# Down-projection of a two-layer decoder trunk: seven pairs of chunks by seven products in two passes

## The chip, the core and the metric

The kernel runs on one core of a Trainium2 chip. TensorE (PE) multiplies, VectorE (DVE), ScalarE (ACT) and GpSimd (POOL) work elementwise, SyncE (SP) and POOL issue DMAs. Every engine takes its instructions in program order and waits on semaphores. The metric is device time in microseconds (us), here the median of three runs: 1158.79 us (1158.62 to 1159.23).

## The reference

A decoder trunk of two layers over 512 tokens of width 1024 in float32: attention, then a gated ConvFFN, each between two RMS norms. What matters here is the ConvFFN, which runs once in each layer:

```
def conv_ffn(xn, w_up, cw, cb, w_down):
    a = xn @ w_up                       # 512 x 5632
    ...                                 # causal depthwise conv of width 3
    gate, val = jnp.split(a, 2, axis=-1)
    return (jax.nn.gelu(gate, approximate=True) * val) @ w_down   # 512 x 2816 @ 2816 x 1024
```

## The kernel before

**Splits.** Each float32 operand is split into a high part (rounded to float32r by ACT) and a low part (operand minus high part, by DVE). A product of two operands is three matmuls (`mm3`, L235 to L238): high by high, high by low, low by high. Class `Weights` (L27) loads weight pieces of 128x1024 in a fixed order (`pieces`), always `ahead_dma` pieces ahead, by DMAs on SP (L41); `high` (L45) is the ACT copy (L49), `low` (L52) the DVE subtraction (L55); `take` hands out pieces that aren't split.

**Up stage.** `ffn` (L509) works through 22 chunks (NF) of 128 rows of the gated width; a chunk needs two pieces of `w_up` (gate and value half). A plain chunk is 48 matmuls of 128x512 (`up`). Chunks in `SEVEN` (6, 8, ..., 20) compute the product of 2x2 blocks by seven products in place of eight: 84 matmuls of 128x256 (`prod`), with sums on DVE (`csum`, L671, L672, and L679 to L686) between them, and `seven_weights` makes their operands two chunks ahead. `weights(c + 2)` is a generator whose steps are put between TensorE's products (`next(steps)`). When TensorE is done with a chunk, `post` runs its taps (`taps`, the convolution: ACT L535, DVE L536 and L538 for each half), the GELU (`glu`, L554), and, a chunk later, `product`, which multiplies gate and value into `hc` and stores it to `hD` in DRAM by a DMA on SP (L549).

**Down projection.** `Proj(NF, 4, get_act).finish` (L322, L351): for each of the 22 chunks (`kc`), for four blocks of 128 tokens (`b`) and two halves of 512 columns (`hf`), `mm3` adds to one of eight PSUM banks (`acc`), which takes all eight banks. A chunk is 24 matmuls of 128x512. The last four chunks are run block by block, so that the boundary (norms, next stage) can start. `load_h` and `prep` (L512, L518) load two chunks of `hD` and split them (`hs`, L523, L524). While chunks 20 and 21 of the up stage run, `weights(22)` and `weights(23)` split the first four pieces of `w_down`, and `prep(0)`, `prep(1)` the first activations.

**Buffers.** `t8` has 17 buffers of 8 KB a partition (split weights `w`, `hs`, `xT`), `t4` 9 of 4 KB (raw weights `wraw`, `bb`, `hraw`), `t2` 6 of 2 KB. A buffer is free for the next tile once all that read or write it is done; the order on each engine is the order of the program.

Of the kernel before, what the change touches and what calls it, by code (L numbers as in the profile page):

```python
# [16 lines left out]
NB = 4  # L17
# [4 lines left out]
EPS = 1e-6  # L22
NEG = -1e30
BIG = 3.0e38


class Weights:  # L27
# [31 lines left out]
    def take(self, k):  # L59

        self.load(self.n_split + k + self.ahead_dma)
        raws = [self.raw.pop(self.n_split + i) for i in range(k)]
        self.n_split += k
        return raws

    def split(self, n):
        while self.n_split < min(n, len(self.pieces)):
# [10 lines left out]
def trunk_kernel(ctx, tc, x, norm_gains, w_qkv_a, w_o_a, w_q_b, w_o_b, kv_norm, w_kvf, b_f,  # L78
# [52 lines left out]
    def add_rows(w, n):  # L131
        for kc in range(n):
            add(lambda raw, kc=kc: [(raw, w[kc * 128:(kc + 1) * 128, :])])

    def add_cols(w, c):
# [2 lines left out]
    def add_ffn(l):  # L138
        for c in range(NF):
            add_cols(w_up[l], c * 128)  # L140
            add_cols(w_up[l], DFF + c * 128)
        add_rows(w_down[l], NF)

    add_rows(w_o_a[0], 6)
    add_ffn(0)
    for hf in range(2):
        for s in range(4):
# [6 lines left out]
                add_cols(w_kvf, c * 128)  # L154
    for c in range(1, 8):
        add_cols(w_q_b[0], c * 128)
    add_rows(w_o_b[0], 8)
    add_ffn(1)

    early = []  # L160
# [100 lines left out]
    class Mix:  # L261


        def __init__(self, gain):
            self.gain, self.st = gain, {}
# [56 lines left out]
    class Proj:  # L322

        def __init__(self, KC, R, get_act):
            self.KC, self.R, self.get_act = KC, R, get_act
            self.w, self.banks, self.done = {}, {}, set()

        def weight(self, kc):  # L330
            while len(self.w) <= kc:
                self.w[len(self.w)] = W.get()
            return self.w[kc]

        def step(self, kc, b, hf, part=slice(0, 512)):
            ah, al = self.get_act(kc)
            w = self.weight(kc)
            s = slice(b * 128, b * 128 + 128)
            c = slice(hf * 512 + part.start, hf * 512 + part.stop)
            if kc == 0:  # L340
                self.banks[b, hf] = bank([128, 512], name="acc")
            mm3(self.banks[b, hf][:, part], ah[:, s], al[:, s], w[0][:, c], w[1][:, c],
                kc == 0, kc == self.KC - 1, part.start > 0)

        def both(self, kc, b):
            if (kc, b) not in self.done:
# [4 lines left out]
        def finish(self, bd, ahead, hook=None):  # L351
            n = self.KC - self.R
            if hook is None:
                for kc in range(n):
# [149 lines left out]

    SEVEN = range(6, NF - 1, 2)

    def ffn(bd, cp, nxt, ahead):  # L509
        hD = tc.dram_tile([NF, 128, T], F32, name="hD")  # L510
# [2 lines left out]
        def load_h(j):  # L513
            if j < NF // 2:
                hraw[j] = t4([128, 2, T], name="hraw")
                sp.dma_start(hraw[j], hD[2 * j:2 * j + 2].rearrange("c p t -> p c t"))

        def prep(j):  # L518
            if j < NF // 2:
                load_h(j + 1)  # L520
                hs[j] = t = t8([128, 2, 2, T], F32R, name="hs")
                src = hraw.pop(j)
                act.copy(t[:, 0], src)  # L523
                dve.tensor_tensor(t[:, 1], src, t[:, 0].bitcast(F32), ALU.subtract)  # L524
# [3 lines left out]
                prep(kc // 2 + 1)  # L528
            return hs[kc // 2][:, 0, kc % 2], hs[kc // 2][:, 1, kc % 2]

        def taps(c, banks):
            bb = t4([128, 2, T], name="bb")
            for s, ch in ((0, c), (1, NF + c)):
                ps = banks[s]
                act.activation(bb[:, s, :], ps, AF.Identity, bias=cp[:, 3, ch:ch + 1], scale=cp[:, 2, ch:ch + 1])  # L535
                dve.scalar_tensor_tensor(bb[:, s, 1:], ps[:, :T - 1], cp[:, 1, ch:ch + 1], bb[:, s, 1:],  # L536
                                         ALU.mult, ALU.add)
                dve.scalar_tensor_tensor(bb[:, s, 2:], ps[:, :T - 2], cp[:, 0, ch:ch + 1], bb[:, s, 2:],  # L538
                                         ALU.mult, ALU.add)
            return bb  # L540

        gated = []

        def product():

            if gated:
                c, bb = gated.pop()
                if c - 1 in hc:
                    sp.dma_start(hD[c - 1], hc.pop(c - 1))  # L549
                hc[c] = t2([128, T], name="hc")  # L550
                dve.tensor_tensor(hc[c], bb[:, 0, :], bb[:, 1, :], ALU.mult)
# [5 lines left out]
        def post(c, banks):  # L557
            product()
            glu(c, taps(c, banks))

        xT = None
        XA, XB = [], []
# [54 lines left out]
        def plain_weights():  # L617
            for _ in range(2):
                W.high()
                W.low()  # L620
                yield

        def weights(c):
            return seven_weights(c) if c in SEVEN else plain_weights()

        def half_mm(o, w, x, s, start):
            for k in range(4):
# [16 lines left out]
        begun = None  # L644
        before = None
        for c in range(2, NF):
            if c == NF - 2:
                load_h(0)
            if c == NF - 1:
                prep(0)  # L650
                prep(1)
            steps = weights(c + 2)
            banks = [bank([128, T], name="up") for _ in range(2)]
            if c in SEVEN:
                w = halves.pop(c)
                W.n_get += 2
                x11, x21, x22 = [(xT[0][i], xT[1][i], s) for i, s in ((0, LO), (1, LO), (1, HI))]
                o1, o2, o3, o4 = banks[0][:, LO], banks[0][:, HI], banks[1][:, LO], banks[1][:, HI]
                s1, s12, s17 = (t2([128, 256], name="csum") for _ in range(3))

                def prod(o, a, x, start=False):
                    half_mm(o, w[a], x[0:2], x[2], start)

                prod(o1, "A11", x11, True)
# [6 lines left out]
                dve.tensor_tensor(s12, o2, s1, ALU.add)  # L671
                dve.tensor_tensor(s17, o3, s1, ALU.add)  # L672
# [12 lines left out]
                next(steps, None)  # L685
                dve.tensor_tensor(o2, o2, s1, ALU.add)  # L686
            else:
                for s in range(2):
                    if s == 0 and begun:
                        w, banks[0] = begun  # L690
                        up(*begun, range(4, KD))
                        begun = None
                    else:
                        up(W.get(), banks[s], range(KD))
                    if s == 0 and before:
                        post(*before)
                    next(steps, None)
                    next(extra, None)
            for _ in steps:
                pass  # L700
            before = c, banks
        post(*before)
        product()
        sp.dma_start(hD[NF - 1], hc.pop(NF - 1))

        W.ahead = 4
        Proj(NF, 4, get_act).finish(nxt, ahead)

# [690 lines left out]
```

## Time and profile before

| | |
|---|---|
| median of three runs | 1158.79 us |
| the profiled execution, time / span | 1158.71 us / 1156.9 us |
| DVE, ACT, POOL busy over the span | 66%, 48%, 11% |
| down projection, layers 0 and 1, first acc matmul | at 419 us and 1033 us |
| DMA, mean over the span | 120 GB/s, 138.90 MB |

A row of the timeline gives start, duration, engine, line and operation, output and inputs; in brackets, how long the engine was idle before it and what it waited for. In a group row, x is the count. A window row gives each engine's busy us (and instructions), the granted clock (PEclk, 1.00 is full), the share of the DMA engines and GB/s.

### The profile page before, as it was taken

The page shows a single profiled execution, that of the slowest core. Times are in us where ns is not written, and L with a number is a line of the kernel's source. Part 1 is how long each engine was busy: PE and PEld are TensorE (multiplying, and loading weights), DVE is VectorE, ACT ScalarE, POOL GpSimd, SP SyncE. Part 2 cuts the span into 40 slices and gives each one's busy share as a digit, 9 for nine tenths or more (in the row PEclk, how much of TensorE's full clock was granted, in tenths as well). Part 3 has the DMA queues.
Part 4 walks back from the last instruction along what each step waited for, and adds up shares of the span by engine and source line. Part 5 has one row for each costly group of instructions (what it writes and reads, how often), then busy time and mean ns, then how long its engine had stood idle before and what let it go on. Part 6 is the DMA issues. An engine that isn't in the chain of part 4 may idle for free.

```text
span 1156.9 us, 16648 instructions
## 1 busy us (share of the span) xinstructions
PE 1142.1 (99%) x6474; PEld 977.5 (84%) x6474; DVE 767.1 (66%) x1227; ACT 554.9 (48%) x956; POOL 131.5 (11%) x191
## 2 busy tenths in 40 slices
PE   9999999999999999999999999999999999999997
PEld 6888889888998888888778888789888998888886
DVE  6433488888878766306564788758788888867204
ACT  5444565444445545305452677755454444445202
POOL 2722003000000000000000565502100000000000
PEclk9999999999999999999999999999999999999999
DMA  8131064334344449203304344274334434539001
GB/s 295 56 111 37 2 173 123 101 110 143 112 127 140 154 158 375 75 1 78 89 1 129 101 118 126 77 203 128 101 92 129 145 105 143 169 124 379 1 1 73
DMA packets 147176, 138.90 MB, mean 120 GB/s; under 512 B 6809, under 2 KB 120969, under 8 KB 147098
## 3 DMA queue, kind: packets, MB, share of 16 engines
q1 hardware_dynamic: 145818, 133.64, 36.7%
q0 software_dynamic: 1280, 4.20, 1.6%
q8 instruction: 51, 0.84, 0.3%
q14 instruction: 27, 0.22, 0.1%
HBM read 119.94 MB, written 13.68 MB: 116 GB/s over the span
## 4 chain that ended last, share of the span: by engine, by line
PE 90%; DVE 4%; ACT 3%; issue 2%; DVEq 0%; ACTq 0%
PE up L236 12%; PE up L237 12%; PE up L238 12%; PE acc L236 9%; PE acc L238 9%; PE acc L237 9%; PE v_ps L236 2%; PE v_ps L238 2%; PE v_ps L237 2%; PE qk_ps L237 2%; PE qk_ps L236 2%; PE qk_ps L238 2%; PE first L238 1%; PE first L236 1%; PE first L237 1%
## 5 line engine op out<-in xcount | busy, mean ns | idle before, releaser
L55 DVE TENSOR_TENSOR w<-wraw,w 128x1024 fp32r<-128x1024 f32 x150 | 189.6, 1279 | 119.2 <-ACT w L49 117.4
L49 ACT CAST w<-wraw 128x1024 fp32r<-128x1024 f32 x150 | 154.2, 1049 | 81.4 <-PE acc L238 56.0
L236 PE MATMUL acc<-w,hs 128*128 128x512 f32 (+1 forms) x356 | 137.9, 387 | 1.1 <-DVE mix L283 1.1
L238 PE MATMUL acc<-w,hs 128*128 128x512 f32 (+1 forms) x356 | 137.6, 387 | 0.0
L237 PE MATMUL acc<-w,hs 128*128 128x512 f32 (+1 forms) x356 | 137.6, 387 | 0.0
L535 ACT ACTIVATE bb<-up,conv 128x512 f32<-128x512 f32 x80 | 60.4, 775 | 149.3 <-DVE up L686 90.9
L236 PE MATMUL up<-xch,w 128*128 128x512 f32 (+1 forms) x288 | 102.2, 355 | 1.7 <-DVE csum L671 1.7
L236 PE MATMUL up<-xbh,w 128*128 128x512 f32 (+1 forms) x288 | 102.1, 355 | 1.7 <-DVE csum L671 1.7
L237 PE MATMUL up<-xcl,w 128*128 128x512 f32 (+1 forms) x288 | 102.0, 354 | 0.0
L237 PE MATMUL up<-xbl,w 128*128 128x512 f32 (+1 forms) x288 | 102.0, 354 | 0.0
L238 PE MATMUL up<-xch,w 128*128 128x512 f32 (+1 forms) x288 | 101.8, 354 | 0.0
L238 PE MATMUL up<-xbh,w 128*128 128x512 f32 (+1 forms) x288 | 101.8, 354 | 0.0
L236 PEld LDWEIGHTS acc<-w,hs 128*128 128x128 f32 x356 | 66.8, 188 | 14.8 <-DVE mix L283 1.3
L237 PEld LDWEIGHTS acc<-w,hs 128*128 128x128 f32 x356 | 66.8, 188 | 13.6
L238 PEld LDWEIGHTS acc<-w,hs 128*128 128x128 f32 x356 | 66.8, 188 | 13.5
L236 PE MATMUL up<-xsh,w 128*128 128x256 f32 x256 | 72.4, 283 | 0.0
L237 PE MATMUL up<-xsl,w 128*128 128x256 f32 x256 | 72.4, 283 | 0.0
L238 PE MATMUL up<-xsh,w 128*128 128x256 f32 x256 | 72.4, 283 | 0.0
L536 DVE SCALAR_TENSOR_TENSOR bb<-up,conv,bb 128x511 f32<-128x511 f32 x80 | 59.4, 743 | 7.2 <-ACT bb L535 7.2
L276 ACT ACTIVATE junk<-acc 128x512 bf16<-128x512 f32 (+1 forms) x33 | 19.2, 582 | 92.4 <-PE acc L238 92.1
L236 PEld LDWEIGHTS up<-xbh,w 128*128 128x128 f32 x288 | 54.4, 189 | 9.5 <-ACT w L49 1.8
L236 PEld LDWEIGHTS up<-xch,w 128*128 128x128 f32 x288 | 54.4, 189 | 9.5 <-ACT w L49 1.8
(273 smaller groups left out, 2662.4 us busy)
## 6 DMA issues: line engine op xcount, KB each, us to landing
wraw<-in_w_up_dram SPq DMA_DIRECT2D x88, 512.0 KB
wraw<-in_w_down_dram SPq DMA_DIRECT2D x44, 512.0 KB
hD<-hc SPq DMA_DIRECT2D x44, 256.0 KB
hraw<-hD SPq DMA_DIRECT2D x22, 512.0 KB
wraw<-in_w_kvf_dram SPq DMA_DIRECT2D x16, 512.0 KB
wraw<-in_w_qkv_a_dram SPq DMA_DIRECT2D x16, 256.0 KB
wraw<-in_w_q_b_dram SPq DMA_DIRECT2D x8, 512.0 KB
ck<-cd SPq DMA_DIRECT2D x8, 512.0 KB
```

The lines of the kernel that those rows point to most:

```text
L49: self.nc.scalar.copy(pair[:, 0], raw)
L55: self.nc.vector.tensor_tensor(pair[:, 1], raw, pair[:, 0].bitcast(F32), ALU.subtract)
L236: pe.matmul(o, ah, bh, start=first, stop=False, skip_group_check=shared)
L237: pe.matmul(o, ah, bl, start=False, stop=False, skip_group_check=shared)
L238: pe.matmul(o, al, bh, start=False, stop=last, skip_group_check=shared)
L276: act.activation(junk[:, :s.stop - s.start], o, AF.Square, scale=1.0 / 32, accum_out=ss[:, n % 2:n % 2 + 1])
L535: act.activation(bb[:, s, :], ps, AF.Identity, bias=cp[:, 3, ch:ch + 1], scale=cp[:, 2, ch:ch + 1])
L536: dve.scalar_tensor_tensor(bb[:, s, 1:], ps[:, :T - 1], cp[:, 1, ch:ch + 1], bb[:, s, 1:], ALU.mult, ALU.add)
```

## The change

The 22 chunks of the down projection are now 14 chunks in seven pairs (ND = 7), and eight plain chunks (14 to 21). A pair is a product of 2x2 blocks (two chunks, two halves of the tokens, two halves of the columns) by seven products: 42 matmuls of 128x512 in place of 48. Pass one does four products of every pair into the eight banks, `combine_one` then mixes the banks in place, and pass two adds the other three. `SEVEN` of the up stage now ends at 18.

Weight pieces of `w_down` come in the order 0 to 13, 14, 15, 1, 3, 16, 17, 5, 7, 9, 11, 13, 18 to 21: the odd chunks of pairs are loaded twice. Some low parts are made by ACT and a DMA: ACT writes the negated, rounded operand, and a DMA on POOL's queue adds the operand to it in place. That is done for the up weights of chunks 20 and 21, for plain chunks 14 and 15 (`high_added`), for one weight operand of pairs 0 to 3 and the activations of pairs 0 and 1 (`pair_highs`); elsewhere DVE subtracts (`pair_lows`). The stores of `hD` go from SP's queue to POOL's. The core of the diff:

```diff
+SEVEN = range(6, 19, 2)
+ND = 7
...
+    def high_added(self):
+        self.load(self.n_split + 1 + self.ahead_dma)
+        raw, pair = self.raw.pop(self.n_split), self.new_pair()
+        self.nc.scalar.copy(pair[:, 0], raw)
+        self.nc.scalar.activation(pair[:, 1], raw, AF.Copy, scale=-1.0)
+        self.nc.gpsimd.dma_start(pair[:, 1], raw, accum_op=ALU.add)
...
-                    sp.dma_start(hD[c - 1], hc.pop(c - 1))
+                    pool.dma_start(hD[c - 1], hc.pop(c - 1))
...
+        def pair_sums(j):
+            pair_load(j + 1)
+            r0, r1 = W.take(2)
+            k = keep[j]
+            t3 = t2([128, 512], name="dt3")
+            dve.tensor_tensor(t3, r1[:, H[1]], r0[:, H[1]], ALU.subtract)
+            dve.tensor_tensor(r0[:, H[1]], r0[:, H[1]], r0[:, H[0]], ALU.subtract)
+            dve.tensor_tensor(k[:, t2_], r1[:, H[1]], r0[:, H[1]], ALU.subtract)
+            dve.tensor_tensor(k[:, s3_], k[:, a11], k[:, s1_], ALU.subtract)
+            dve.tensor_tensor(k[:, s1_], k[:, s1_], k[:, a22], ALU.add)
+            dve.tensor_tensor(k[:, s2_], k[:, s1_], k[:, a11], ALU.subtract)
+            sums[j] = r0, t3
+
+        def pair_highs(j):
+            r0, t3 = sums.pop(j)
+            k = keep[j]
+            wa, wb, ac = one[j] = [t8([128, 2, 1024], F32R, name="w") for _ in range(3)]
+            act.copy(wa[:, 0], r0)
+            if j < 4:
+                act.activation(wa[:, 1], r0, AF.Copy, scale=-1.0)
+                pool.dma_start(wa[:, 1], r0, accum_op=ALU.add)
+            act.copy(wb[:, 0, H[1]], t3)
+            act.copy(wb[:, 0, H[0]], k[:, t2_])
+            act.copy(ac[:, 0], k[:, 0:1024])
+            if j < 2:
+                act.activation(ac[:, 1], k[:, 0:1024], AF.Copy, scale=-1.0)
+                pool.dma_start(ac[:, 1], k[:, 0:1024], accum_op=ALU.add)
+            lows[j] = k, t3, wb, ac, wa, r0
+
+        def pair_lows(j):
+            k, t3, wb, ac, wa, r0 = lows.pop(j)
+            if j >= 4:
+                dve.tensor_tensor(wa[:, 1], r0, wa[:, 0].bitcast(F32), ALU.subtract)
+            dve.tensor_tensor(wb[:, 1, H[1]], t3, wb[:, 0, H[1]].bitcast(F32), ALU.subtract)
+            dve.tensor_tensor(wb[:, 1, H[0]], k[:, t2_], wb[:, 0, H[0]].bitcast(F32), ALU.subtract)
+            if j >= 2:
+                dve.tensor_tensor(ac[:, 1], k[:, 0:1024], ac[:, 0].bitcast(F32), ALU.subtract)
...
+        def pair_two(j):
+            r1, = W.take(1)
+            k = keep.pop(j)
+            w, ac = (t8([128, 2, 1024], F32R, name="w") for _ in range(2))
+            t4p = t4([128, 2, 512], F32R, name="wsum")
+            act.copy(w[:, 0], r1)
+            dve.tensor_tensor(k[:, t2_], r1[:, H[0]], k[:, t2_], ALU.subtract)
+            dve.tensor_tensor(k[:, s2_], k[:, a12], k[:, s2_], ALU.subtract)
...
+        def mul_one(j, bp):
+            wa, wb, ac = one[j]
+            for key, q, w, c in (((bp, 0), 0, wa, H[0]), ((bp, 1), 3, wb, H[0]),
+                                 ((bp + 2, 0), 2, wb, H[1]), ((bp + 2, 1), 1, wa, H[1])):
+                if j == 0:
+                    db[key] = bank([128, 512], name="acc")
+                product_of(db[key], ac, q, w, c, bp, j == 0)
...
+        def down_pairs(po):
+            n = 2 * ND
+            pair_highs(3)
+            for bp in range(2):
+                for j in range(2):
+                    mul_one(j, bp)
+            for j in range(1, ND - 2):
+                if j > 1:
+                    mul_one(j, 0)
+                    mul_one(j, 1)
+                if j + 3 < ND:
+                    pair_sums(j + 3)
+                    pair_lows(j + 2)
+                    pair_highs(j + 3)
+                    if j + 3 == ND - 1:
+                        load_h(ND)
+                elif j + 3 == ND:
+                    pair_lows(j + 2)
+                if j == ND - 3:
+                    W.high_added()
+            W.high_added()
+            prep(ND)
+            for bp in range(2):
+                for j in (ND - 2, ND - 1):
+                    mul_one(j, bp)
+                combine_one(bp)
...
+                    for kc in (n, n + 1):
+                        for b in (bp, bp + 2):
+                            po.both(kc, b)
...
                     if s == 0 and before:
-                        post(*before)
+                        post(*before, (lambda: pair_lows(0)) if c == NF - 1 else None)
+                        if c >= NF - 2:
+                            pair_highs(c - NF + 2)
+                            pair_sums(c - NF + 3)
...
+            if c == NF - 3:
+                pair_sums(0)
-        post(*before)
+        post(*before, lambda: pair_lows(1))
+        pair_highs(2)
+        pair_sums(3)
+        pair_lows(2)
```

`between` is called in `taps` after the first half of a chunk, so `pair_lows(1)` stands on DVE between the two halves of chunk 21's taps. `combine_one(bp)` reads four banks: two ACT copies and four DVE additions of 512 columns. Pass two runs plain chunks 14 and 15 first, then pairs 0 and 1, chunks 16 and 17, and pairs 2 to 6, with `pair_two` of a pair (its five DVE and three ACT instructions) two pairs ahead; chunks 18 to 21 are the last four, as before.

More of the change, by code (lines that the diff above doesn't have):

```diff
@@ L129, in trunk_kernel, with add_rows @@
         add(lambda raw, s=s: [(raw.rearrange("p (k c) -> p k c", k=2), cols(wqkv, 2 * s, 2, 1792, 512))])
-    def add_rows(w, n):
-        for kc in range(n):
+    def add_rows(w, chunks):
+        for kc in chunks:
             add(lambda raw, kc=kc: [(raw, w[kc * 128:(kc + 1) * 128, :])])
@@ L353, in finish @@
             if hook is None:
-                for kc in range(n):
+                for kc in range(self.begin, n):
                     for b in range(NB):
@@ L539, in taps @@
                                          ALU.mult, ALU.add)
+                if s == 0 and between is not None:
+                    between()
             return bb
@@ new lines, in ffn, with pair_load @@
+        keep, one, two = {}, {}, {}
+        H = slice(0, 512), slice(512, 1024)
+        a11, s1_, s3_, s2_, a12, a22 = (slice(i * 256, i * 256 + 256) for i in range(6))
+        t2_ = slice(1536, 2048)
+        def pair_load(j):
+            if j < ND:
+                keep[j] = k = t8([128, 2048], name="dkeep")
+                sp.dma_start(k[:, 0:512], hD[2 * j])
+                sp.dma_start(k[:, 1024:1536], hD[2 * j + 1])
+        def pair_sums(j):
[10 more added lines that the diff above has]
+            sums[j] = r0, t3
@@ new lines, in combine_one, with mul_two @@
+        def combine_one(bp):
+            a, b, c, d = db[bp, 0], db[bp, 1], db[bp + 2, 0], db[bp + 2, 1]
+            p1, u, u3 = (t2([128, 512], name="dsum") for _ in range(3))
+            act.copy(p1, a)
+            dve.tensor_tensor(u, b, p1, ALU.add)
+            dve.tensor_tensor(c, c, u, ALU.add)
+            act.copy(u3, c)
+            dve.tensor_tensor(b, d, u, ALU.add)
+            dve.tensor_tensor(d, d, u3, ALU.add)
+        def mul_two(j, bp):
+            ac, w, t4p = two[j]
+            product_of(db[bp, 0], ac, 1, w, H[0], bp, False)
+            product_of(db[bp + 2, 0], ac, 2, t4p, H[0], bp, False)
+            product_of(db[bp, 1], ac, 0, w, H[1], bp, False)
@@ new lines, in run @@
+        def run(steps):
+            for _ in steps:
+                pass
+        def down_pairs(po):
[18 more added lines that the diff above has]
+                    W.high_added()
+            W.high_added()
+            prep(ND)
[3 more added lines that the diff above has]
+                combine_one(bp)
+            one.clear()
+            W.n_get += n
+            pair_two(0)
+            for bp in range(2):
+                for kc in (n, n + 1):
+                    for b in (bp, bp + 2):
+                        po.both(kc, b)
+            pair_two(1)
+            for j in range(ND):
+                if j == 2:
+                    W.n_get += 2
+                    pair_two(j + 1)
+                    for kc in (n + 2, n + 3):
+                        for b in range(NB):
+                            po.both(kc, b)
+                if j == 1:
+                    W.split(W.n_split + 1)
+                    W.split(W.n_split + 1)
+                    pair_two(2)
+                if 2 <= j < ND - 2:
+                    pair_two(j + 2)
+                if j == ND - 1:
+                    W.n_get += ND - 2
+                if j >= ND - 2:
+                    W.split(W.n_split + 2)
+                for bp in range(2):
+                    mul_two(j, bp)
+                del two[j]
@@ L646, in ffn @@
         for c in range(2, NF):
[L647 to L652, printed above, removed]
+            if c == NF - 4:
+                pair_load(0)
+            steps = weights(c + 2) if c + 2 < NF else iter(())
             banks = [bank([128, T], name="up") for _ in range(2)]
```

58 lines of the change are left out of this document (37 added, 21 removed).

## The prediction

> **What bounds the kernel now.** I read the page's head and its chain of waits first, then the windows by stage in the first ConvFFN, then the waits, then the timeline of each engine around the place that changes.
>
> ```profile
> span 1156.9 us, 16648 instructions
> PE 1142.1 (99%) x6474; PEld 977.5 (84%) x6474; DVE 767.1 (66%) x1227; ACT 554.9 (48%) x956; POOL 131.5 (11%) x191
> ...
> PE 90%; DVE 4%; ACT 3%; issue 2%; DVEq 0%; ACTq 0%
> ```
>
> TensorE is the bound: 90% of the chain that ended last is its own work. So a matmul taken out is worth its full slot, as long as the operands of the next one are there. The windows (up stage, then three thirds of the down projection of layer 0) say how much room the others have.
>
> ```profile
> core 0: us, PE busy (x) PEld busy (x) DVE busy (x) ACT busy (x) POOL busy (x), PEclk, DMA share, GB/s
> 360.00:390.00 30.00, 30.00 (x190) 27.25 (x190) 24.23 (x35) 13.41 (x18) 0.00 (x0) 1.00 0.45 134
> 419.00:450.00 31.00, 31.00 (x139) 25.66 (x138) 26.30 (x25) 20.20 (x21) 0.00 (x0) 1.00 0.84 316
> 450.00:480.00 30.00, 30.00 (x134) 24.85 (x133) 10.02 (x9) 9.01 (x9) 0.00 (x0) 1.00 0.63 216
> 480.00:510.00 30.00, 30.00 (x134) 24.82 (x134) 6.03 (x5) 4.28 (x5) 0.00 (x0) 1.00 0.00 1
> ```
>
> TensorE never waits in any of them. VectorE (DVE) has 24 of 30 us in the up stage and is nearly empty later in the down projection: the change moves work into that room, but not evenly. The early window is the one to watch.
>
> **Slot of a matmul.** The busy time of a row (389 ns) overlaps its neighbour's; the slot is the distance of starts. In the timeline of the down projection and in the chain of waits inside a chunk of seven products:
>
> ```profile
> 499.77 0.39 PE L238 MATMUL acc<-w,hs 128*128 128x512 f32 x1
> ...
> 502.94 0.39 PE L237 MATMUL acc<-w,hs 128*128 128x512 f32 x1
> ```
> ```profile
> 396.35 0.12 PE up L236
> ...
> 399.11 0.14 PE up L238
> 399.24 0.02 issue
> ...
> 400.74 1.02 issue
> 401.76 0.43 DVE csum L671
> 402.19 0.14 issue
> 402.32 0.36 PE up L236
> ```
>
> From 499.77 to 502.94 are 14 steps: 0.2264 us; over ten such stretches I get 0.2267 and use it. The 256-wide ones take 23 steps from 396.35 to 399.11, 0.120 each, so a bit more than half.
>
> **Part A, products taken out.** Eight block products of a pair of chunks become seven. A product is two token blocks by three matmuls, so a pair needs 42 in place of 48. Seven pairs in two layers: 7 x 2 x 6 = 84 matmuls of 128x512, 84 x 0.2267 = 19.0 us. That is the whole of what can be won from them.
>
> **Part B, chunk 20 of the up stage.** SEVEN also loses its last member (20). A plain chunk is 48 x 0.2267 = 10.88 us, one of seven products 84 x 0.1204 = 10.11: plus 0.77 a layer, 1.5 us in all.
>
> **Part C, a wait that goes.** The chain above shows TensorE idle from 400.66 to 402.32 in chunk 20. There the first product's sum (csum, L671) stands on DVE behind a low part (L55) that waits for ScalarE's (ACT's) high part. The list of waits has it once in each layer:
>
> ```profile
> PE up L236 <- DVE csum L671: 3.3, 2, 1.7
> ```
>
> Chunk 18 is now the last of seven products, and the weight steps between its sums are `high_added`: two ACT instructions and a DMA, none on DVE. So the sum no longer stands behind a wait, and chunk 20 has no such sum. Minus 3.3 us; zero if something else holds that place.
>
> **Part D, pass one against the vector queue.** Here the price lies. Distances of starts on DVE at the end of layer 0's up stage (copies of 1024, 512 and 256 columns, and the taps, L536/L538) and on ACT in layer 1:
>
> ```profile
> 401.76 0.42 DVE L671 TENSOR_TENSOR csum<-up,csum 128x256 f32<-128x256 f32 x1
> 402.09 0.41 DVE L672 TENSOR_TENSOR csum<-up,csum 128x256 f32<-128x256 f32 x1
> 402.42 1.22 DVE L55 TENSOR_TENSOR w<-wraw,w 128x1024 fp32r<-128x1024 f32 x1
> ...
> 419.81 0.69 DVE L551 TENSOR_TENSOR hc<-bb 128x512 f32<-128x512 f32 x1
> 420.41 0.74 DVE L536 SCALAR_TENSOR_TENSOR bb<-up,conv,bb 128x511 f32<-128x511 f32 x1
> ...
> 423.47 0.69 DVE L551 TENSOR_TENSOR hc<-bb 128x512 f32<-128x512 f32 x1
> 424.08 1.22 DVE L55 TENSOR_TENSOR w<-wraw,w 128x1024 fp32r<-128x1024 f32 x1
> 425.22 1.22 DVE L524 TENSOR_TENSOR hs<-hraw,hs 128x1024 fp32r<-128x1024 f32 x1
> ```
> ```profile
> 1033.36 1.03 ACT L49 CAST w<-wraw 128x1024 fp32r<-128x1024 f32 x1
> 1034.31 1.04 ACT L523 CAST hs<-hraw 128x1024 fp32r<-128x1024 f32 x1
> 1035.25 1.04 ACT L49 CAST w<-wraw 128x1024 fp32r<-128x1024 f32 x1
> ```
>
> DVE: 0.33 for 256 columns, 0.61 for 512, 1.14 for 1024, 3.06 for the four taps of a chunk. `pair_sums` is three of 512 and three of 256, two of them on the result just before: 3.0 us. `pair_lows` is 1.2 for pairs 0 and 1 (two of 512; the rest by adding DMAs), 2.4 for 2 and 3, 3.5 for 4 to 6. A pair in pass one is 24 matmuls, 5.44 us. So from pair 4 on DVE needs 6.5 us for each 5.44 of TensorE, and it starts in debt, because chunk 21's taps stand among the pairs' steps.
>
> I walk the queue with zero where chunk 21's last matmul slot ends (419.08 in layer 0, the start of the first acc matmul). The taps started 1.3 after that before; now ACT comes from `pair_highs(1)`, so 1.5. Then DVE: taps 3.06, lows(1) 1.2, sums(3) 3.0, lows(2) 2.4, the gate's product 0.6 (11.8); sums(4), lows(3) 5.4 (17.2); sums(5), lows(4) 6.5 (23.7); sums(6), lows(5) 6.5 (30.2); lows(6) 3.5 (33.7), with half a microsecond for two waits on ACT 34.2. TensorE's order puts pair 6 of the first token half before everything of the second half: its third matmul needs the last low part, and 34 slots, 7.7 us, follow. Pass one ends at 41.9; without waits it would end at 168 x 0.2267 = 38.1. That is 3.8 us lost a layer. With whole durations for distances (1.22, 0.69, 0.42) the walk ends pass one at 44.2, 6.1 lost.
>
> ```profile
> 419.08 0.39 PE L236 MATMUL acc<-w,hs 128*128 128x512 f32 x1
> ```
>
> The other late operand is pair 1's low part by an adding DMA. The taps of chunk 20 can start at -10.9, are held up by lows(0) in their middle, and end at -5.5; the gate's GELU and then `pair_highs(1)` follow on ACT: at 0.95 each of 1024 columns and about half that of 512, its first adding DMA is issued near -2 and its second (the activations) near 0.9. TensorE asks for the second at 3.2, after 14 slots. If the add takes d from issue to landing, TensorE waits d - 2.3. No row shows an adding DMA. The nearest is POOL's copy inside SBUF of half the bytes, the second of two in a row:
>
> ```profile
> L1138 POOL DMA_DIRECT2D qst<-qst x8: 509/510/517, 639.7 to 729.6; - x8
> ...
> DMA to landing us min/median/max: 3.5/3.6/4.8
> ```
>
> Bounds: 3.5 if the bytes cost nothing (wait 1.2), 9.6 if it is twice the longest (wait 7.3). I take twice the median, 7.2, as the bytes double and loads run beside it: wait 4.9. The two losses don't add: while TensorE waits for the add, DVE goes on and its debt shrinks. The larger counts, so I take 5.0 a layer, 10.0 in all, with 3.8 and 7.3 as ends. No page prices this add directly; the Trainium skill, "DMA: Bandwidth & Descriptors" (Anatomy of one DMA), gives 2.0 us plus bytes over 436 GB/s, and "Collectives: The Full Stack" (The bandwidth ceiling) says that an add reads two sources, so my estimate from both is 2.0 + 2 x 1.2 = 4.4 us, and by it the DVE walk alone would set the loss, about 1147 us.
>
> **Edits costed at nothing.** Stores of the gated rows go from SP's queue to POOL's: POOL has 0.00 us busy in 360 to 390, so about half a microsecond of issue each is covered; uncovered it would delay only stores that are read tens of microseconds later. Behind them in POOL's queue stand the adds: the store of chunk 21 waits for DVE's product near 12.4, and add(3) behind it is due only near 20. SP's queue now holds the pair loads: `pair_load(5)` waits for a buffer that pair 0 leaves, near 11, and the weights behind it are for pair 5, due at 17. Bytes: a pair in pass one loads 1.5 MB in 5.44 us, 290 GB/s; the stretch of loads in the old down projection had
>
> ```profile
> DMA packets 3098, 8.76 MB, mean 398 GB/s; under 512 B 270, under 2 KB 270, under 8 KB 3097
> ```
>
> so the loads fit, and the seven odd chunks read a second time fall where the windows show 216 and 1 GB/s. At 398 GB/s a pair's bytes take 3.9 of its 5.44 us; only loads slower than 280 GB/s would make TensorE wait. ACT in pass one has 2.9 us a pair, 0.95 more for each add. `combine_one` of the first half lies under 24 matmuls of the second half, that of the second under the 24 of plain chunks 14 and 15; uncovered, some 3.5 us each. Pass two needs 3.6 us of DVE a pair (1.14 + 0.61 + 0.33 + 0.61 + 0.86) against 18 x 0.2267 = 4.08, with 96 plain matmuls between: no wait. Adds of up weights 20 and 21 are issued a whole chunk, over 10 us, ahead.
>
> **Sum.** Against the profiled execution's own 1158.71 us (span 1156.9, and 1.8 around it): -19.0 + 1.5 - 3.3 + 10.0 = -10.8, so 1147.9; the median of the runs is 0.08 above it: 1148.0. The likeliest case's own range, with Part D from 3.8 to 7.3 a layer: 1145 to 1153.
>
> **Rivals.**
>
> First: *no debt on DVE*. If the sums and lows interleave better than my walk (taps of 21 start earlier, adds land in 3.5), pass one loses 1 us a layer or none: 1158.8 - 19.0 + 1.5 - 3.3 + 0 to 2 = 1138 to 1140. For it: DVE is at 24 of 30 us and has free time in chunks 20 and 21. Against: 33 us of DVE work counted above lie behind one tap that can't be earlier.
>
> Second: *the wait cools TensorE*. Rows first:
>
> ```profile
> 400.66:402.32 1.66, 0.00 (x1) 0.03 (x1) 1.66 (x3) 1.66 (x3) 0.00 (x0) 1.00 0.59 227
> 1150.00:1156.90 6.90, 1.21 (x11) 1.00 (x9) 1.91 (x4) 0.77 (x3) 0.00 (x0) 0.82 0.20 76
> ```
> ```profile
> 1.35 1.89 PE warm L197 x4
> ```
>
> An idle of 1.66 us kept the granted clock at 1.00; in the last stretch, nearly idle, it fell to 0.82; and the first matmuls after a start took 1.89 / 4 = 0.47 us, twice the slot. If pair 1's wait of 4.9 us crosses that point, some 16 matmuls run at 0.47: 4 us more a layer, partly while DVE is in debt anyway; say 2 of them count: 1152. The Trainium skill, "TensorE: Matmul & The Clock Gate" (Rules for kernel authors), states the point: no gaps above about 3 us between bursts, or the clock halves. The row of 1.66 agrees with it, and no run here shows a gap of 3 to 5 us amid matmuls. Against it in the walk: the wait is in two parts with matmuls between.
>
> Third, on the other side: *the adding DMA is slow*. Place: the two adds of pair 1 in each layer. Each microsecond of d above 7.3 costs one. Gains outside D are 20.8, 10.4 a layer, so the change loses from d = 12.7 on, 3.5 times the row of half the bytes. At d = 15 the wait is 12.7 and pair 0's add is late too, perhaps 1 more: 1158.8 + 2 x 3.3 = 1165. For it: no row shows such a DMA, and the loads of pairs 3 and 4 (2.5 MB, 6 us at 398 GB/s) fall on the same engines then. Against: the row's spread is 3.5 to 4.8.
>
> Fourth: *near nothing*. DVE's instructions run 20% longer beside the adds and loads: the walk's 34 us become 41, 11 lost a layer: 1160. Against: the 512-column rows beside loads at 316 GB/s keep 0.69.
>
> **How the numbers follow.** Forecast (1145 to 1151) 0.48; no debt 0.10; moderate loss, the cooling or d near 9 (1151 to 1156.5) 0.23; slow adds 0.10; the long DVE 0.09, half of it within 0.2%, which is 2.3 us and about what a measurement of this kernel can tell from no change. So faster 0.81, same 0.05, slower 0.14. For 8 times in 10 the range runs from 1141 to 1158: it leaves out most of "no debt" and the two slow cases.
>
> **What would show it.** In the changed kernel: TensorE's waits list no csum of 1.7; in the 42 us behind the last up matmul TensorE is idle about 5 us a layer, first on an adding DMA of pair 1, then on low parts of pairs 4 to 6; DVE is busy over 90% there and under 80% in pass two, where TensorE has no gap; the adds land in 5 to 9 us; PEclk stays 1.00. The prediction is wrong if the idle time there is under 2 us or over 8, if pass two waits, or if the 512-wide slot isn't 0.227.

## The result, and the profile after

The changed kernel takes 1152.68 us (median of four runs, 1151.64 to 1154.04) against 1158.74 for the kernel before on the same chip: ratio 0.9948, 95% interval 0.9930 to 0.9965. That is 6.1 us faster; 10.8 were forecast (1148.0), and the range of 1141 to 1158 holds it.

The page of the changed kernel, its head and its chain of waits:

```profile
span 1152.3 us, 16764 instructions
...
PE 1128.4 (98%) x6318; PEld 960.0 (83%) x6318; DVE 832.0 (72%) x1365; ACT 609.1 (53%) x1038; POOL 176.3 (15%) x259
...
PE 81%; DVE 8%; issue 4%; ACT 3%; DMA 3%; SPq 0%; DVEq 0%; POOL 0%; POOLq 0%; ACTq 0%
```

TensorE's own work fell from 90% to 81% of the chain; VectorE has 8% of it, and the DMAs 3%, where they had no share to speak of. What it waits for, from the list of waits (total us, times, longest):

```profile
PE acc L254 <- DVE w L703: 4.9, 5, 1.8
PE acc L254 <- DMA w<-dkeep: 2.9, 2, 1.8
PE o_ps L1482 <- ACT pT L1469: 2.8, 3, 1.5
PE acc L253 <- DMA w<-wraw: 2.3, 1, 2.3
...
PE acc L253 <- DVE w L699: 0.8, 1, 0.8
```

The csum wait of 3.3 is gone, as forecast. Four new rows stand under `acc`, 10.9 us in nine waits: on adding DMAs (`w<-dkeep` are activations, `w<-wraw` weights) and on low parts made by VectorE (L699, L703).

To find the time, the kernel is cut where TensorE changes its work. First the two matmuls of the kernel before that the prediction doesn't show, then the same cuts of the changed kernel, with one wait between:

```profile
205.62 0.40 PE L236 MATMUL up<-xbh,w 128*128 128x512 f32 x1
...
530.60 0.27 PE L431 MATMUL xt_ps<-ident,xn 128*128 128x128 f32 x1
```
```profile
205.78 0.40 PE L252 MATMUL up<-xbh,w 128*128 128x512 f32 x1
...
418.11 0.39 PE L252 MATMUL acc<-w 128*128 128x512 f32 x1
...
435.80 0.39 PE L252 MATMUL acc<-w 128*128 128x512 f32 x1
438.48 0.50 PE L253 MATMUL acc<-w 128*128 128x512 f32 x1 [2.29 <-DMA w<-wraw]
438.82 0.39 PE L254 MATMUL acc<-w 128*128 128x512 f32 x1
...
527.80 0.27 PE L448 MATMUL xt_ps<-ident,xn 128*128 128x128 f32 x1
```

The up stage of layer 0 went from 213.46 to 212.33 (B and C together: -1.13), the down projection from 419.08 to 530.60, 111.52, to 109.69. By part A it should have lost 42 x 0.2267 = 9.52 and stand at 102.00; so 7.7 us are lost in it, and by the same cuts 7.5 in layer 1 (before 121.06, after 119.01, from its first `acc` matmul, which stands at 1029.87 before and not at 1033 as the table of the time before has it, up to the last matmul). The rows also show what a wait costs: the distance 435.80 to 438.48 is 2.68, a loss of 2.45 for an idle of 2.29, and the next distance, 0.34, loses another 0.11. So each wait costs its idle time plus about 0.27.

The profiled execution took 1154.04, 1.4 over the median. The attention between the two ConvFFNs, which the change doesn't touch, is 1.4 longer than in the profile before (from the end of this cut to the next `up` matmul; the row `o_ps` has three waits where the kernel before has one of 1.5); in the repeat of the same kernel below it is as before. Over all profiles this stretch runs from 285.5 to 287.6 us, so differences of up to 2 us between two medians are read with the cuts beside them.

### The profile page after: what moved, and what is told of

It reads as the page before. It is cut to its first block, busy times and chain, and to the rows that moved or that the text cites. A ratio compares the mean times of both kernels' runs of the same rounds, so it can differ in the third digit from the quotient of the medians.

```text
span 1152.3 us, 16764 instructions
## 1 busy us (share of the span) xinstructions
PE 1128.4 (98%) x6318; PEld 960.0 (83%) x6318; DVE 832.0 (72%) x1365; ACT 609.1 (53%) x1038; POOL 176.3 (15%) x259
## 4 chain that ended last, share of the span: by engine, by line
PE 81%; DVE 8%; issue 4%; ACT 3%; DMA 3%; SPq 0%; DVEq 0%; POOL 0%; POOLq 0%; ACTq 0%
PE up L253 11%; PE up L252 11%; PE up L254 11%; PE acc L254 7%; PE acc L252 7%; PE acc L253 7%; PE v_ps L252 2%; PE v_ps L254 2%; PE v_ps L253 2%; DMA wraw<-in_w_down_dram 2%; PE qk_ps L253 2%; PE qk_ps L252 2%; PE qk_ps L254 2%; PE first L254 1%; PE first L252 1%
## 5 line engine op out<-in xcount | busy, mean ns | idle before, releaser
L59 DVE TENSOR_TENSOR w<-wraw,w 128x1024 fp32r<-128x1024 f32 x114 | 145.5, 1296 | 66.2 <-ACT w L53 65.4
L53 ACT CAST w<-wraw 128x1024 fp32r<-128x1024 f32 x114 | 116.5, 1048 | 26.0 <-DMA wraw<-in_w_down_dram 8.7
L252 PE MATMUL up<-xbh,w 128*128 128x512 f32 (+1 forms) x292 | 104.8, 359 | 0.0
L254 PE MATMUL up<-xbh,w 128*128 128x512 f32 (+1 forms) x292 | 104.7, 359 | 0.0
L570 POOL DMA_DIRECT2D hD<-hc x42 | 26.2, 624 | 316.5 <-DVE hc L572 316.5
L254 PE MATMUL acc<-w 128*128 128x512 f32 x168 | 66.9, 398 | 7.8 <-DVE w L703 4.9
L253 PE MATMUL acc<-w 128*128 128x512 f32 x168 | 66.3, 395 | 3.1 <-DMA w<-wraw 2.3
L252 PE MATMUL acc<-w 128*128 128x512 f32 x168 | 66.0, 393 | 0.0
L254 PE MATMUL up<-xsh,w 128*128 128x256 f32 x224 | 63.4, 283 | 0.0
L252 PE MATMUL up<-xsh,w 128*128 128x256 f32 x224 | 63.4, 283 | 0.0
L253 PE MATMUL up<-xsl,w 128*128 128x256 f32 x224 | 63.4, 283 | 0.0
L252 PEld LDWEIGHTS up<-xbh,w 128*128 128x128 f32 x292 | 55.1, 189 | 8.3
L254 PEld LDWEIGHTS up<-xbh,w 128*128 128x128 f32 x292 | 55.1, 189 | 8.2
L557 DVE SCALAR_TENSOR_TENSOR bb<-up,conv,bb 128x510 f32<-128x510 f32 x80 | 59.9, 749 | 2.8
L253 PEld LDWEIGHTS up<-xbl,w 128*128 128x128 f32 x292 | 55.1, 189 | 8.1
```

Of the source, the lines that this page charges most:

```text
L53: self.nc.scalar.copy(pair[:, 0], raw)
L59: self.nc.vector.tensor_tensor(pair[:, 1], raw, pair[:, 0].bitcast(F32), ALU.subtract)
L252: pe.matmul(o, ah, bh, start=first, stop=False, skip_group_check=shared)
L253: pe.matmul(o, ah, bl, start=False, stop=False, skip_group_check=shared)
L254: pe.matmul(o, al, bh, start=False, stop=last, skip_group_check=shared)
L570: pool.dma_start(hD[c - 1], hc.pop(c - 1))
```

## The experiments

Eleven kernels were run, each beside the kernel before (1158.76 to 1158.92 in the medians of the batches). "Lost" is the down projection's length, cut as above, less 102.00 in layer 0 and less 111.54 in layer 1.

| kernel | median us | ratio to before, 95% | lost, layer 0 / 1 |
|---|---|---|---|
| changed kernel again | 1152.38 | 0.9945 [0.9933, 0.9958] | 8.0 / 6.7 |
| raws first | 1150.32 | 0.9921 [0.9908, 0.9935] | 4.7 / 7.2 |
| pairs on DVE | 1145.69 | 0.9887 [0.9873, 0.9900] | 4.0 / 3.9 |
| adds left out | 1145.67 | 0.9888 [0.9872, 0.9903] | 3.6 / 3.9 |
| low part later (kernel before) | 1155.21 | 0.9971 [0.9960, 0.9982] | |
| late adds on DVE | 1147.70 | 0.9901 [0.9885, 0.9918] | 6.5 / 4.5 |
| adds on 4 and 5 | 1143.33 | 0.9867 [0.9852, 0.9882] | 1.9 / 1.9 |
| only 14, 15 added | 1150.10 | 0.9926 [0.9912, 0.9941] | 5.8 / 5.8 |
| adds on 4 and 5, raws first | 1142.08 | 0.9854 [0.9840, 0.9869] | 1.6 / 1.6 |
| adds on 3 and 5 | 1150.55 | 0.9929 [0.9914, 0.9944] | 5.3 / 6.7 |
| adds on 4, 5 and 6 | 1155.14 | 0.9963 [0.9949, 0.9977] | 8.0 / 9.2 |

Two theories were set against each other. *The queue* ("debt" in the expectations): pass one loses what VectorE's debt costs, and the adds are worth what they take from it. *The transfers* ("loads" and "latency" there): the adding DMAs themselves cost time, as they hold the DMA engines, so that raw weights come late and the adds land late.

**The changed kernel again**, unaltered, as the yardstick of its batch.

> The changed kernel once more, as the yardstick on the chip of the runs beside it. Theories: (1) loads: the adding DMAs fill the DMA engines, the raw weights come late and DVE's sums starve (6.0 us idle before the sums of pair 5 in layer 0); (2) debt: DVE simply has too much to do, as the prediction walked it; (3) latency: TensorE waits for the adds themselves (1.1 + 2.3 us in layer 0); (4) order: SP's queue stands at the load of a pair's activations, which waits for a buffer, and the raw weights behind it are issued late. All expect 1152 to 1154.

1152.38. The single waits fall elsewhere (in layer 0 now 1.70 and 1.84 on L699 and L703), their sum hardly.

**Raws first.** In `pair_sums` the raw weights are handed out, and the loads that this frees issued, before the next pair's activations, whose buffer comes free late:

```diff
-            pair_load(j + 1)
             r0, r1 = W.take(2)
+            pair_load(j + 1)
```

> The raw weights of the next pair are issued ahead of the load that waits for a buffer. Order (4): the raws of pair 5 are issued about 7 us earlier, DVE's wait of 6.0 us for them falls under 2, the kernel gains 4 to 8 us on the changed one: 1145 to 1149. Loads (1): the DMA engines are busy all the time from 400 to 445 us and the bytes are the same, so the wait only moves: within 2 us of the changed kernel. Debt (2) and latency (3): no difference.

2.1 us gained, less than *order* had and about the limit of *loads*. VectorE waits only 0.3 and 1.5 us for raw weights, but TensorE now waits 2.84 and 3.33 for the adds of pair 1's activations; in layer 1 slow matmuls behind that wait took back what was won. The order on SP's queue is a part of the loss, and the smaller one.

**Pairs on DVE**: no pair uses an adding DMA; VectorE makes every low part of the pairs.

```diff
-            if j < 4:
+            if j in ():
...
-            if j < 2:
+            if j in ():
```

(and `j not in ()` for the two subtractions of `pair_lows`)

> The low parts of pairs by DVE alone: six adding DMAs a layer go, six subtractions of 1.14 us come, four of them while the up stage still runs. Debt (2): 2.3 to 6.8 us more of DVE work a layer on the path, so 1157 to 1166. Loads (1): DVE's wait for raw weights is gone, the loss in pass one falls from 7.4 to about 4 a layer: 1145 to 1149. Latency (3): the waits on adds (3.9 a layer with the restart) go, the DVE work comes: 1150 to 1157.

1145.69, 7 us less than the changed kernel, although VectorE has six more subtractions of 1024 columns in each layer. Only one kind of row under `acc` is left in its list of waits:

```profile
PE acc L254 <- DVE w L703: 5.6, 6, 1.3
```

5.6 + 6 x 0.27 = 7.2, 3.6 a layer: this is VectorE's debt alone. Two views of it beside the changed kernel's say why it is faster. The DMA engines from 400 to 445 us (queue, packets, MB, share of the 16 engines), changed kernel first:

```profile
q1 hardware_dynamic: 3061, 8.60, 53.1%
q0 software_dynamic: 1407, 4.95, 49.0%
```
```profile
q1 hardware_dynamic: 3291, 9.43, 58.8%
q0 software_dynamic: 531, 1.78, 13.0%
```

q0 is POOL's queue. It moved 3.17 MB less, the six adds of 0.52 MB, and was busy (0.490 - 0.130) x 45 = 16.2 us less: 2.7 us of all 16 engines for each add. The loads on q1 took 0.588 x 45 = 26.5 us for 9.43 MB, so 1.47 for the same bytes. And the windows from 418 to 442, changed kernel first:

```profile
418.00:442.00 24.00, 20.63 (x90) 16.43 (x89) 16.19 (x27) 13.96 (x19) 2.89 (x4) 1.00 1.00 315
```
```profile
418.00:442.00 24.00, 22.71 (x100) 18.19 (x98) 22.83 (x35) 13.44 (x18) 0.54 (x1) 1.00 0.75 271
```

With the adds the DMA engines are at 1.00 and VectorE stands idle for 8 of 24 us; without them the engines are at 0.75, VectorE works 22.8 us, and ten more matmuls get done. The time lies in the range of *loads* and far from that of *debt*.

**Adds left out.** The lines of `pair_highs` that issue the two adding DMAs are gone; the addition of the pairs' operands (six of 512 KB in each layer) is left out, and VectorE doesn't do it either.

```diff
-                pool.dma_start(wa[:, 1], r0, accum_op=ALU.add)
...
-                pool.dma_start(ac[:, 1], k[:, 0:1024], accum_op=ALU.add)
```

> Leaves out the adding DMAs of the pairs (the low parts keep the negated rounded operand), with all of ACT's and DVE's instructions kept. Debt (2): DVE's queue is as long as before, loss in pass one 4 to 6 a layer: 1147 to 1150. Latency (3): only the direct waits go, 3.9 a layer, and DVE's wait for raw weights stays near 6: 1144 to 1147. Loads (1): both go, the wait for raw weights falls under 1 us and the loss under 2.5 a layer: 1140 to 1143.

1145.67, the same as with all of it on VectorE. That is in the range of *latency*, but VectorE's wait for raw weights didn't stay near 6; and it misses the range of *loads*, which put the rest at under 2.5 a layer, where 3.6 and 3.9 were left. So the relief that the six adds give VectorE is worth nothing there: in the first pairs it has time, as it meets late raw weights anyway, by this row of its timeline:

```profile
434.46 0.69 DVE L671 TENSOR_TENSOR dt<-wraw 128x512 f32<-128x512 f32 x1 [1.87 <-DMA wraw<-in_w_down_dram]
```

In the changed kernel the same wait is 6.03, and the raw weights land 4.3 us later:

```profile
431.47 1.22 DVE L703 TENSOR_TENSOR w<-dkeep,w 128x1024 fp32r<-128x1024 f32 x1
438.72 0.69 DVE L671 TENSOR_TENSOR dt<-wraw 128x512 f32<-128x512 f32 x1 [6.03 <-DMA wraw<-in_w_down_dram]
```

The debt that sets the loss is made behind this point, in pairs 4 to 6, which have no adds.

**Low part later**: the kernel before, with each low part of a plain chunk's weights one step later. It has part C without the rest.

```diff
-            for _ in range(2):
-                W.high()
-                W.low()
-                yield
+            W.high()
+            yield
+            W.low()
+            W.high()
+            yield
+            W.low()
```

> The kernel before, with one edit: in the plain weight steps a low part comes one step after its high part, so that DVE doesn't wait for ACT ahead of the sum of chunk 20. It isolates Part C. As the prediction has it: TensorE's wait of 1.7 us on the sum is gone in both layers, 3.3 us less than before: 1155.2 to 1156. Rival: the low part now stands before a later sum, or the wait has another cause: 1158 to 1159.

1155.21, 3.55 less than before. Its up stage is cut by

```profile
206.01 0.40 PE L236 MATMUL up<-xbh,w 128*128 128x512 f32 x1
...
417.65 0.39 PE L236 MATMUL acc<-w,hs 128*128 128x512 f32 x1
```

211.64, 1.82 less than before: the idle 1.66 and the restart. The changed kernel's 212.33 is 0.69 longer, which is part B.

**Late adds on DVE**: weight adds for pairs 0 and 1 only (the activations' adds of pairs 0 and 1 stay).

```diff
-            if j < 4:
+            if j in (0, 1):
```

> The changed kernel with the weight lows of pairs 2 and 3 by DVE; the adds of pairs 0 and 1 stay. DVE's queue behind the up stage grows by 2.3 us a layer. Loads, with the harm done by the adds in pass one itself: DVE's wait for raw weights falls to 2 or 3 us, TensorE's wait on the weight add of pair 3 goes: 1148 to 1150.5. Loads, with the harm done by the backlog of the four adds before it: wait for raws still 5 or more, longer DVE queue: 1151.5 to 1155.

1147.70, 5.0 of the 7 us (0.3 under the first range), and VectorE's wait for raw weights fell to 2.6 and 0.6 us. The two adds issued while pass one runs (pairs 2 and 3) do most of the harm.

**Adds on 4 and 5**: the weight adds move to the pairs in which VectorE has its debt, and all others go to VectorE.

```diff
-            if j < 4:
+            if j in (4, 5):
...
-            if j < 2:
+            if j in ():
```

> The low parts of pairs 0 to 3 by DVE, two adding DMAs a layer for the weights of pairs 4 and 5, where TensorE waits on DVE's low parts when all pairs are on DVE (losses of 1.3, 1.3 and 0.6 us a layer, and 0.1 at each restart). Debt alone is left: DVE's queue gets 2.3 us a layer shorter, loss 1 to 2 a layer in place of 3.7: 1140 to 1142.5. Loads: the DMA engines are at 0.95 from 428 to 440 us already, two adds of some 3 us of all engines make the raws of pairs 5 and 6 late again: 1146 to 1150. Latency: an add lands in 7 us, pair 5's after TensorE asks for it: 1144 to 1147.

1143.33, 9.4 less than the changed kernel and between the ranges: the loss of 1.9 a layer is what *debt alone* said, the time is 0.8 over it. VectorE is relieved of two times 1.14 us a layer where it counts, and the loss falls by 2.1 and 1.9 against "pairs on DVE".

**Only 14, 15 added**: as "pairs on DVE", and the up weights of chunks 20 and 21 are split by VectorE too.

> All pairs on DVE, and the up weights of chunks 20 and 21 too (low parts one step after the high parts): of twelve adding DMAs a layer the two of plain chunks 14 and 15 are left. If the adds of the up weights cost nothing, as the prediction had it: as with the pairs on DVE alone, 1145 to 1146.5. If their traffic delays loads for pass one: 1143 to 1144.5. If DVE falls behind at the end of the up stage without them: 1147 to 1150.

1150.10, 4.4 slower than "pairs on DVE":

```profile
PE acc L254 <- DVE w L708: 8.8, 8, 1.7
```

The down projections lose 3.7 of the 4.4; the rest lies outside them. VectorE falls behind at the end of the up stage: its sums of pair 3 start at 422.32 where they start at 420.44 in "pairs on DVE". So the adds of the up weights pay. They run in a stage where the DMA engines have room (share 0.53 from 380 to 404 us without them, 0.89 with them).

**Adds on 4 and 5, raws first** joins the two that helped.

> The pairs add on 4 and 5 alone, and the raw weights of a pair are loaded before the next pair's activations. If what is left there (1.1 to 1.3 us a layer in 'adds on 4 and 5') is partly VectorE waiting for late raw weights, this saves up to 1 us a layer: 1141.5 to 1143. If it only moves the wait to the activations, as it did in 'raws first' (4.3 us on the stores' rows), the time stays at 1143 to 1145.

1142.08, the fastest of all: 16.8 less than before. Its down projections are only 0.3 a layer shorter than with adds on 4 and 5 alone; the cuts don't show where the rest of the 1.25 us between the medians comes from. Under `acc` its list of waits has

```profile
PE acc L253 <- DMA w<-wraw: 1.4, 2, 1.0
...
PE acc L254 <- DVE w L703: 0.3, 1, 0.3
```

**Adds on 3 and 5** and **adds on 4, 5 and 6** ask when an add may be issued; only the two tuples of the diff above differ.

> The weight adds of pairs 3 and 5 in place of 4 and 5. By the theory of transfers (adds hurt while loads run beside them) the earlier add of pair 3 falls among the loads of pairs 4 and 5, so they land later and TensorE waits 1 to 2 us a layer more: 1144.5 to 1147. By the theory of the queue alone (only VectorE's debt counts, and pair 3's subtraction lies before pair 4's) the earlier relief is the better one: 1142 to 1143.5.

> A third weight add, for pair 6. VectorE is relieved of another 1.14 us a layer, but the add is issued last and TensorE asks for its result soon after. If it lands in 7 to 8 us, as those of pairs 4 and 5, TensorE waits for it instead of VectorE: 1143 to 1146. If the last low parts of VectorE are what is left, it gains up to 0.6 a layer: 1142 to 1143.

1150.55 and 1155.14, both outside every range named: against adds on 4 and 5 they lose 7.2 and 11.8 us. The first, ACT's timeline (the operand of pair 3's add), POOL's and TensorE's:

```profile
423.18 1.06 ACT L686 ACTIVATE w<-wraw 128x1024 fp32r<-128x1024 f32 x1
428.20 0.54 POOL L895 DMA_DIRECT2D hD<-hc  x1 [13.89 <-DVE hc L572]
428.82 0.89 POOL L687 DMA_DIRECT2D w<-wraw  x1
```
```profile
438.00 0.50 PE L253 MATMUL acc<-w 128*128 128x512 f32 x1 [3.39 <-DMA w<-wraw]
```

and the second:

```profile
444.73 0.86 POOL L687 DMA_DIRECT2D w<-wraw  x1 [5.91 <-ACT w L688]
```
```profile
452.48 0.80 PE L253 MATMUL acc<-w 128*128 128x512 f32 x1 [3.16 <-DMA w<-wraw]
```

Pair 3's add is out 9.2 us before TensorE can go on, pair 6's 7.8; TensorE was ready 3.4 and 3.2 us earlier. By the queue alone the add for pair 3 should have been the better one; it was the worse by 7.2 us. Its loss isn't all the transfers': ACT was done with the operand at 424.24, but the add stands behind chunk 21's store (L895) in POOL's queue, which waits for VectorE's product, and went out 4.6 us later, more than TensorE waited for it; in layer 1 it is 4.6 again, for a wait of 4.30. Pair 3's add ahead of that store was not run, so what it would cost there stays open. The expectation for the third add was too mild: beside the wait itself, 14 slow matmuls followed (see the clock below).

## Why the forecast held in direction and was off by half in size

**A held.** Where little is lost, "adds on 4 and 5, raws first", 3.2 us are lost in both layers, and the three waits shown explain 1.7 + 3 x 0.27 = 2.5 of them; 0.35 a layer are left for anything else.

**B held** (0.69 a layer for 0.77), and **C held** (1.82 a layer for 1.66): the wait went, and its restart with it.

**D was mis-sized: 15.2 us in place of 10.0.** With -19.0, +1.4 and -3.7 this gives -6.1, the measured difference. The first thing missing is a term: the sum counts a wait at its idle time. TensorE's idle time came out close to the forecast, 10.9 us for 10.0; but nine restarts of 0.27 put 2.4 on top and the slow clock in layer 1 some 1.7, and with both 15.0 of the 15.2 are accounted for. That the idle time came out close is luck, as it is made up differently: 5.2 on adds and 5.7 on VectorE, where 9.8 on adds alone was forecast.

The step of the mechanism that failed is "The two losses don't add: while TensorE waits for the add, DVE goes on and its debt shrinks. The larger counts". With its restarts, VectorE's debt alone costs 3.6 to 4.0 a layer, as the walk said (3.8); the adds put 3.7 to 4.4 on top in layer 0 and 2.8 to 3.6 in layer 1, over both profiles of the changed kernel. VectorE doesn't go on while TensorE waits: it stands for 6.03 us itself, for raw weights. The reason is a second sentence, "so the loads fit". It counted the bytes of the loads and none of the adds, which hold the engines for 2.7 us each; with them the engines' share is 1.00 where it would be 0.75. How much of this is the late raw weights and how much the adds' own lateness shifts from one execution to the next; "raws first" turned one into the other and got back 2 of 7.

**The add's own wait** was wrong in both of its terms. d was 8.4 us or more for the activations (7.2 taken, 3.5 to 9.6 as ends),

```profile
L693 POOL DMA_DIRECT2D w<-dkeep x4: 845/845/847, 403.8 to 1023.0; - x4
...
DMA to landing us min/median/max: 8.4/10.3/11.7
```

but POOL issued it 4.0 us before the first `acc` matmul (418.11), where the walk has 0.9 after it:

```profile
414.09 0.84 POOL L693 DMA_DIRECT2D w<-dkeep  x1 [2.31 <-ACT w L692]
```

So the wait on it was 1.1 and 1.8, not 4.9. The walk had put the taps of chunks 20 and 21 behind the last matmul of each. The taps of a first half need only the first bank and ran before that, and so `pair_highs(1)` and VectorE's low parts of pair 1 started some 5 us earlier, and its sums of pair 3 at 420.57, 2.5 us after the first `acc` matmul, where the walk has 5.8. That the debt came out as walked is therefore in part luck: it began smaller, and VectorE then lost the time to the raw weights (1.87 even with the adds left out). The Trainium skill, "DMA: Bandwidth & Descriptors" (Anatomy of one DMA) and "Collectives: The Full Stack" (The bandwidth ceiling), gave my estimate of 4.4 us, which no add of the pairs reached (7.0 was the fastest in the changed kernel, 5.6 in all runs); the add of plain chunk 14 in the changed kernel (L76, at 452.45) came close with 4.5. The Trainium skill's rule that an add reads two sources agrees in kind with the 2.7 against 1.47 us of the engines.

**Edits at nothing.** `combine_one` and pass two cost nothing, by the windows of the changed kernel:

```profile
419.00:450.00 31.00, 26.36 (x114) 20.85 (x113) 24.00 (x38) 17.53 (x24) 2.89 (x4) 1.00 0.95 313
450.00:480.00 30.00, 28.44 (x125) 22.90 (x124) 26.80 (x36) 18.07 (x23) 1.73 (x2) 1.00 0.64 168
480.00:510.00 30.00, 30.00 (x134) 24.85 (x133) 24.59 (x29) 18.02 (x21) 0.00 (x0) 1.00 0.60 192
...
1055.00:1058.00 3.00, 3.00 (x9) 2.34 (x8) 2.81 (x7) 2.00 (x3) 0.00 (x0) 0.55 0.57 190
```

They show pass two (480 to 510) without a gap, with VectorE at 82%, a little over the 80% named. Three marks failed: VectorE at over 90% in pass one (24.00 of 31, 77%, as it waited), PEclk at 1.00 throughout (last row), and adds landing in 5 to 9 us (those of the pairs took 7.0 to 11.7). The mark of TensorE's idle time, about 5 us a layer, held: 6.2 and 4.7.

The move of the stores to POOL's queue held up an add. The prediction had pair 3's add behind chunk 21's store "due only near 20"; TensorE asked for it 18.1 us after the first `acc` matmul and waited 2.29. ACT had written its operand by 425.38, and the store ahead of it let it out at 427.89, 2.5 us later:

```profile
424.33 1.05 ACT L686 ACTIVATE w<-wraw 128x1024 fp32r<-128x1024 f32 x1
```
```profile
427.27 0.56 POOL L895 DMA_DIRECT2D hD<-hc  x1 [4.04 <-PE acc L254]
427.89 0.90 POOL L687 DMA_DIRECT2D w<-wraw  x1
```

Other adds follow ACT in some 0.3 us (pair 4's in "adds on 4 and 5"). Whether this one, let out earlier, would have landed earlier among the loads, no run shows.

**Rivals.** *No debt* didn't happen here; moving the adds to pairs 4 and 5 comes near it. *The wait cools TensorE* came partly true, by shorter waits than walked, and cost about 1.7 us in this profile (in layer 1, seven matmuls 0.2 slower each, the rest in those around them). *The adding DMA is slow*: the pairs' weight adds landed in 7.0 to 10.5 us, activations in 8.4 to 11.7, under the 12.7 at which it would have decided alone; its price came through the engines that it holds. *The long DVE* is out: the 512-column rows still take 0.69.

## What to carry to other kernels

An adding DMA that takes work off a busy engine isn't free: count it in the DMA engines' time, here at nearly twice a load of its size, and in the stage in which it runs, not over the kernel. Issue it well over its landing time under load ahead of its reader (8 to 10 us here), for the operands where the relieved engine really is in debt, and look at what stands before it in the queue that issues it. Count a wait at more than its idle time: each restart cost 0.27 us here. When two waits feed one engine, they only overlap if nothing couples them; ask whether the first one's cause also starves the second.

## What the runs showed of the hardware that was not expected

TensorE's granted clock fell after waits that were short, and not always. "Late adds on DVE", TensorE in layer 0:

```profile
423.65 0.50 PE L254 MATMUL acc<-w 128*128 128x512 f32 x1 [2.20 <-DMA w<-dkeep]
...
424.97 0.63 PE L252 MATMUL acc<-w 128*128 128x512 f32 x1
425.40 0.63 PE L253 MATMUL acc<-w 128*128 128x512 f32 x1
```

After 2.20 us of idling the slot went to 0.43 (424.97 to 425.40) for some 3 us. "Raws first" idled longer at the same place and kept its slot of 0.23:

```profile
424.05 0.50 PE L254 MATMUL acc<-w 128*128 128x512 f32 x1 [2.84 <-DMA w<-dkeep]
424.38 0.39 PE L252 MATMUL acc<-w 128*128 128x512 f32 x1
424.61 0.40 PE L253 MATMUL acc<-w 128*128 128x512 f32 x1
```

The clock also fell after two waits with one matmul between (0.79 and 1.84 in the changed kernel, 1.70 and 1.84 in its repeat) and after every wait of 3.1 us or more (five of them in "raws first" and the last two kernels). The gap of about 3 us that the Trainium skill names, "TensorE: Matmul & The Clock Gate" (Why this matters for your kernels), is thus the right size but no safe bound: two shorter waits with a matmul between them sufficed twice, and one of 2.2 us once. The slow stretch lasted 7 to 14 matmuls, 1.6 to 3 us on top of the wait and its restart. Which other condition decides between 2.2 and 2.84 was not tried.
